# Attention values computed in pairs of column blocks, with some of their products in the seven-product form, and a new order of the stages around them

## The chip, the cores and the metric

The kernel runs on one core of a Trainium2 chip. The metric is the device time of one execution in microseconds (us). Three runs of the kernel before gave 2039.58, 2039.71 and 2039.95 us; the median, 2039.71 us, is the time to which the changed kernel is compared.

## The reference, cut to what matters

One layer of a hybrid block on x of 256 rows by 4096 columns, all in float32:

```
xn   = rms_norm(x)
proj = xn @ w_in                 # 4096 -> 14336: q, k, v, z_a, a_c, g_c, z_c, 2048 columns each
y_a  = attention(q, k, v)        # 16 heads of 128; here every query row sees the earlier chunks; a bias from rel_table
y_a  = rms_norm(y_a) * silu(z_a)
u    = a_c * sigmoid(g_c)
u    = depthwise_conv(u, 31 taps) # along the rows, channel by channel
y_c  = silu(layer_norm(u)) @ w_pw
y_c  = rms_norm(y_c) * silu(z_c)
h    = x + [y_a, y_c] @ w_out
h    = h + sigmoid(rms_norm(h) @ w_ple_gate + b) * (p @ w_ple)
out  = rms_norm(h)
```

## The kernel before, in words

**Products.** Every large product has 256 output rows (two halves of 128, called h), blocks of 512 output columns, and a depth of 4096 in 32 blocks of 128. To keep float32 accuracy each operand is split in a high part and a low part, and each product is made of three matmuls: high by high, low by high, high by low. The left operand (`xT`, transposed and split once) stays in memory; each weight block comes by DMA into a tile `wt` and is split there (`parts_of`, lines 199 to 209): ScalarE casts the high part (`wh`, line 204) and VectorE subtracts it from the weight to get the low part (`wl`, line 205).

There are two routines. `product` (line 224) makes one block of 512 columns: 32 depth blocks, two halves, three matmuls, so 192 matmuls (line 218). `mixed_product` (line 327) makes two column blocks at once and takes the depth in 16 pairs of blocks; an `order` says in which sequence and which pairs are "seven" pairs, marked with a star. A plain pair takes 24 matmuls, from two split weight tiles of 128x1024. A seven pair is a step of a Strassen-like scheme: seven products of 128-blocks in place of eight, 21 matmuls. It needs sums of weight blocks, `ua` and `ub` (VectorE, lines 426, 427, 430, 431), which are split as well (`uh`, `ul`, again lines 204 and 205), and combinations of left blocks that were made earlier. Four helper banks (P1, P5, P6, P7, shown as `acc_P`) are added up by VectorE after the last seven pair (`helper_sums`, lines 467 to 471). `scaled_pair` (line 478) wraps `mixed_product`: it takes two tiles `z` from `sum_tiles` (line 473, tag "stage"), puts the helpers' sums in, scales them, and at the end adds the four accumulators with four VectorE instructions (line 492).

**Stages.** The first third of the kernel makes, from `w_in`, for c and g from 0 to 3:

- `glu_conv(c)` (line 689): a `scaled_pair` for a_c and g_c, a sigmoid and a product, transposes, and 124 convolution taps of VectorE (`conv_tap`, lines 671 to 680), which are not issued but put into a list `later`;
- `heads(g)` (line 883): a DMA of the bias of four heads and a memset on GpSimd, a `scaled_pair` for queries and keys, `to_heads` (line 826: transposes into `qT` and `kT`, tag "hd"), one `product` for the values (line 903, two ScalarE copies at line 904), and `attention` (line 844), head after head, which writes into a new tile `y_a` (tag "act");
- `layer_norm_swish` (line 726), whose 71 steps (four idle ones among them at three places) also go into `later`.

The order is glu_conv(0), glu_conv(1), heads(0), glu_conv(2), heads(1), glu_conv(3), heads(2), layer_norm_swish, heads(3). Of glu_conv(3) six pairs are seven pairs (`early_six`, line 321), of the other pairs from glu_conv(1) on four (`early`, line 320). Then `w_pw` follows (line 956, order "1 3 4 5 0* 6 2* 7" for its first two column blocks); its operand `uS` is made by the last 16 steps of the layer norm.

**What sets the order.** Each product calls `fill(n)` after each pair (line 419 or 457; `product` at line 235, two for each two depth blocks), which takes n steps off `later`. `early_fills` (line 323) gives these numbers pair by pair; they add up to 64. The place at which a step is taken off gives its place in the program. A scheduler orders each engine's queue at compile time: it takes the ready instruction that stands first in the program, so later taps come forward where an engine would be idle. On the chip each queue runs in that fixed order. Tiles come from pools with tags: a tag has a fixed number of buffers (weight parts `wh` and `wl` 3 each, `uh` and `ul` 2 each, "hd" 5, the small PSUM tiles 4). The scratch pool `upool` is closed in heads(3) behind the keys, and a pool `more`, for `uS`, takes its place (lines 898 to 900). The pool `spool` is closed before `w_pw`, and `lpool` takes its place (line 937): from it come `ua` and `ub` of `w_pw` and its row of b_pw.

Of the kernel before, what the change touches and what calls it, by code (L numbers as in the profile page):

```python
# [25 lines left out]
def hybrid_block(  # L26
# [137 lines left out]
    def transposed(src, blocks, then=lambda ins: None):  # L164

        pt = tmp_psum()
        for i, b in enumerate(blocks):
            for h in range(NH):
                last_transpose[:] = [
                    nc.tensor.transpose(  # L170
                        pt[:, i * T + h * P : i * T + (h + 1) * P],
                        src[:, h, b * P : (b + 1) * P],
                        ident,
                    )
                ]
                then(*last_transpose)
        return [pt[:, i * T : (i + 1) * T] for i in range(len(blocks))]
# [143 lines left out]
    early_six = units("1 3 5 7 0* 9 2* 11 4* 13 6* 15 8* 10* 12 14")  # L321

# [175 lines left out]
    def square_sum(dst, src, scale=1.0):  # L498
        junk = spool.tile([P, NB], mybir.dt.bfloat16, tag="junk", name="junk", bufs=1)
        return nc.scalar.activation(junk[:, : src.shape[1]], src, AF.Square, scale=scale, accum_out=dst)  # L500
# [225 lines left out]
    def layer_norm_swish():  # L726
# [4 lines left out]
        def hd_tile(name):  # L731
            return spool.tile([P, 4, T], F32, tag="hd", name=name, bufs=5)

# [92 lines left out]
    def to_heads(st, name):  # L826

        t = spool.tile([P, GH, T], F32, tag="hd", name=name, bufs=5)
# [15 lines left out]
    def attention(g, qT, kT, v, bias):  # L844
        y = act.tile([P, NH, NB], F32, tag="act", name="y_a")
        for hd in range(GH):
# [28 lines left out]
            for h in range(NH):  # L875
                nc.scalar.activation(
                    y[:, h, vc], o[:, h * HD : (h + 1) * HD], AF.Identity, scale=den[:, h : h + 1]
                )
        for h in range(NH):
            square_sum(ssq_a[:, h, g : g + 1], y[:, h, :])  # L880
        y_a.append(y)

    def heads(g):
        nonlocal more
        bias = spool.tile([P, GH, T], F32, tag="hd", name="bias", bufs=5)
# [10 lines left out]
        q, k = scaled_pair(w_in0, o_q + g * NB, o_k - o_q, early, r_x, (4,) if g == n_g - 1 else early_fills)  # L896
        qT, kT = to_heads(q, "qT"), to_heads(k, "kT")
        if g == n_g - 1:
            first_sums.close()
            more = pool("more", 4)  # L900
        accv = product(w_in0, o_v + g * NB, xT, KD)
        v = spool.tile([P, NH, NB], F32, tag="hd", name="v", bufs=5)
        for h in range(NH):
            nc.scalar.activation(v[:, h, :], accv[h], AF.Identity, scale=r_x[:, h : h + 1])
        attention(g, qT, kT, v, bias)

    n_g = H // GH
    assert n_g == CW // NB
# [68 lines left out]
    def gated(ys, c0, col, r_y, order, ahead):  # L977
# [8 lines left out]
        for h, j in QUARTERS:  # L986
            zz, y = z[h][j], ys[c0 + j][:, h, :]
            tt(zz, acc[h][j], zz, ALU.subtract if j else ALU.add)
            nc.scalar.activation(zz, zz, AF.Silu, scale=r_x[:, h : h + 1])
            later.append(partial(stt, y, y, r_y[:, h : h + 1], zz, ALU.mult, ALU.mult))  # L990
# [280 lines left out]
```

## Time and profile before

| what | value |
|---|---|
| runs, median | 2039.71 us |
| the profiled execution, first to last instruction | 2038.9 us |
| TensorE (PE): busy, matmuls | 2021.0 us, 9106 |
| VectorE (DVE): busy | 1905.7 us |
| ScalarE (ACT): busy | 1184.3 us |
| GpSimd (POOL): busy | 8.1 us |
| read from device memory | 406.39 MB |

The profile has no total of its own for the profiled execution beyond its span; the median of the runs is 0.8 us above that span. PE stands for matmuls and PEld for the loads of their stationary operand. A matmul's duration in the profile has a modelled end; matmuls overlap, so the rate at which they follow each other is read from the chain, as its time divided by its count. VectorE's instructions overlap a little too, so a step's cost there is the distance between two starts.

### The profile page before, as it was taken

The numbers are of one execution on the slowest core, as the hardware profiler recorded it, in microseconds if no ns is written. First come the engines' busy times: TensorE is split into PE (matmuls) and PEld (weight loads), VectorE is DVE, ScalarE is ACT, GpSimd is POOL, SyncE is SP. The second block draws the span as 40 slices with busy tenths as digits, with TensorE's granted clock in tenths as the row PEclk, the third lists the DMA queues.
The fourth block names the chain that finished last, engine by engine and source line by source line (L and its number), as shares of the span: only waits on it lengthen the run. The fifth ranks groups of instructions, "written<-read, shape, count | busy, mean of one in ns | idle before, by whom it ended". The sixth has DMA issues, their size and how long they took to land.

```text
span 2038.9 us, 26038 instructions
## 1 busy us (share of the span) xinstructions
PE 2021.0 (99%) x9106; PEld 1661.3 (81%) x9106; DVE 1905.7 (93%) x2720; ACT 1184.3 (58%) x1527; POOL 8.1 (0%) x19
## 2 busy tenths in 40 slices
PE   9999999999999999999999999999999999999997
PEld 7888888887888888888888888888888888888876
DVE  7999999899989998878899999999999999999998
ACT  7655535554555545576555656676565666655555
POOL 0000000000000000000000000000000000000000
PEclk9999999999999999999999999999999999999999
DMA  8566665666656665556666666676666656666765
GB/s 294 188 198 204 200 191 167 203 191 186 184 178 211 202 184 186 178 192 197 187 216 206 197 214 201 215 243 204 211 205 205 206 190 208 198 222 205 234 206 180
DMA packets 161853, 412.29 MB, mean 202 GB/s; under 512 B 12974, under 2 KB 16190, under 8 KB 161722
## 3 DMA queue, kind: packets, MB, share of 16 engines
q1 hardware_dynamic: 161072, 409.80, 62.9%
q8 instruction: 71, 1.16, 0.2%
q10 hardware_dynamic: 650, 0.84, 0.1%
q14 instruction: 60, 0.49, 0.1%
HBM read 406.39 MB, written 4.19 MB: 201 GB/s over the span
## 4 chain that ended last, share of the span: by engine, by line
PE 86%; DVE 10%; issue 2%; ACT 1%; DMA 0%; POOLq 0%; POOL 0%; ACTq 0%; DVEq 0%
PE acc L370 60%; PE acc_P L370 15%; PE acc L218 8%; DVE wl L205 4%; DVE cv L677 3%; PE tmp_ps L170 1%; DVE ul L205 1%; ACT wh L204 0%; PE tmp_ps L834 0%; PE tmp_ps L849 0%; DVE ub L431 0%; PE tmp_ps L867 0%; DVE ub L430 0%; DVE ua L426 0%; DVE ua L427 0%
## 5 line engine op out<-in xcount | busy, mean ns | idle before, releaser
L370 PE MATMUL acc<-wh,big_t 128*128 128x512 f32 x3788 | 1173.6, 391 | 0.9 <-DVE y_c L964 0.7
L204 ACT CAST wh<-wt 128x1024 fp32r<-128x1024 f32 (+1 forms) x737 | 714.7, 980 | 558.4 <-PE acc L370 335.4
L205 DVE TENSOR_TENSOR wl<-wt,wh 128x1024 fp32r<-128x1024 f32 (+1 forms) x737 | 823.7, 1130 | 48.2 <-ACT wh L204 43.0
L370 PEld LDWEIGHTS acc<-wh,big_t 128*128 128x128 f32 x3788 | 708.2, 188 | 147.9 <-DVE y_c L964 1.1
L370 PE MATMUL acc<-wl,big_t 128*128 128x512 f32 x1894 | 730.7, 391 | 0.2 <-DVE wl L205 0.2
L370 PEld LDWEIGHTS acc<-wl,big_t 128*128 128x128 f32 x1894 | 355.2, 188 | 75.7 <-DVE wl L205 2.0
L677 DVE SCALAR_TENSOR_TENSOR cv<-uT,dw,cv 128x255 f32<-128x255 f32 (+20 forms) x480 | 205.1, 463 | 1.3
L204 ACT CAST uh<-ub 128x1024 fp32r<-128x1024 f32 x122 | 128.3, 1052 | 123.9 <-DVE ub L431 99.9
L218 PE MATMUL acc<-wh,big_t 128*128 128x512 f32 x560 | 173.9, 392 | 0.0
L204 ACT CAST uh<-ua 128x1024 fp32r<-128x1024 f32 x122 | 128.6, 1054 | 72.5 <-DVE ua L427 65.3
L205 DVE TENSOR_TENSOR ul<-ub,uh 128x1024 fp32r<-128x1024 f32 x122 | 148.8, 1219 | 7.7 <-ACT uh L204 6.9
L370 PE MATMUL acc_P<-uh,big_t 128*128 128x512 f32 x504 | 154.4, 392 | 0.1
L205 DVE TENSOR_TENSOR ul<-ua,uh 128x1024 fp32r<-128x1024 f32 x122 | 148.6, 1218 | 0.6 <-ACT uh L204 0.4
L218 PEld LDWEIGHTS acc<-wh,big_t 128*128 128x128 f32 x560 | 105.5, 189 | 21.6
L370 PEld LDWEIGHTS acc_P<-uh,big_t 128*128 128x128 f32 x504 | 93.5, 188 | 22.3 <-ACT uh L204 3.6
L218 PE MATMUL acc<-wl,big_t 128*128 128x512 f32 x280 | 109.6, 392 | 0.0
L426 DVE TENSOR_TENSOR ua<-wt 128x512 f32<-128x512 f32 x122 | 83.7, 686 | 26.3 <-DMA wt<-in_w_in_dram 21.4
L370 PE MATMUL acc_P<-ul,big_t 128*128 128x512 f32 x252 | 96.5, 391 | 0.0
L427 DVE TENSOR_TENSOR ua<-wt 128x512 f32<-128x512 f32 x122 | 83.4, 684 | 4.6 <-DMA wt<-in_w_in_dram 3.5
L431 DVE TENSOR_TENSOR ub<-ub,wt 128x512 f32<-128x512 f32 x122 | 83.6, 685 | 1.0
L430 DVE TENSOR_TENSOR ub<-ua,wt 128x512 f32<-128x512 f32 x122 | 83.4, 683 | 0.3
L370 PE MATMUL acc<-uh,big_t 128*128 128x512 f32 x244 | 75.4, 390 | 0.0
(241 smaller groups left out, 1526.4 us busy)
## 6 DMA issues: line engine op xcount, KB each, us to landing
wt<-in_w_in_dram SPq DMA_DIRECT2D x447, 512.0 KB, 4.1
wt<-in_w_out_dram SPq DMA_DIRECT2D x128, 512.0 KB, 4.1
wt<-in_w_ple_gate_dram SPq DMA_DIRECT2D x128, 512.0 KB, 4.2
wt<-in_w_pw_dram SPq DMA_DIRECT2D x32, 512.0 KB, 4.6
hc<-in_x_dram SPq DMA_DIRECT2D x8, 512.0 KB, 5.6
wt<-in_w_ple_dram SPq DMA_DIRECT2D x8, 512.0 KB, 4.4
xin<-in_x_dram SPq DMA_DIRECT2D x7, 512.0 KB, 8.3
out_dram<-hc SPq DMA_DIRECT2D x12, 256.0 KB, 2.5
```

Source lines behind the costliest of these rows:

```text
L170: nc.tensor.transpose(pt[:, i * T + h * P : i * T + (h + 1) * P], src[:, h, b * P : (b + 1) * P], ident,)
L204: nc.scalar.copy(wh[:, :kc, :], wt[:, :kc, :]),
L205: nc.vector.tensor_tensor(wl[:, :kc, :], wt[:, :kc, :], wh[:, :kc, :].bitcast(F32), ALU.subtract),
L218: nc.tensor.matmul(acc, a, b[:, k, :], start=kb == 0 and kind == 0, stop=kb == kblocks - 1 and kind == 2,)
L370: nc.tensor.matmul(banks[name], a, b, start=name not in begun, stop=final and ends[name] == n and kind == 2 and not (left and name in "P2 ...
L426: plus(ua[:, 0], w0[:, 0], w0[:, 1])
L427: plus(ua[:, 1], w0[:, 1], w1[:, 1])
L430: plus(ub[:, 0], ua[:, 0], w1[:, 1])
L431: plus(ub[:, 1], ub[:, 0], w1[:, 0])
L677: nc.vector.scalar_tensor_tensor(cv[:, i, PAD - k :], uT[:, i, : T + k - PAD], dw[:, b, k : k + 1], cv[:, i, PAD - k :], ALU.mult, ALU.add,)
```

## The change

It does these things:

- `values(g, ...)` makes the values of two column blocks (8 heads) with one `scaled_pair`: 16 pairs, 4 of them seven pairs. values(0) has `early` and `early_fills`, values(2) a new order `valued` and fills of its own (their sum is 58). The values then lie in the tiles `z`, for values(0) with the tag "hd", for values(2) "stage".
- `qT` is taken from the pool "act", and attention writes its result over it, head by head; the squares and the later readers take it as a tile of four dimensions.
- The order is glu_conv(0), glu_conv(1), bias 0, keys(0), values(0), attention(0), glu_conv(2), glu_conv(3), bias 1, keys(1), attention(1), keys(2), layer_norm_swish, keys(3), values(2), attention(2), attention(3).
- Biases 2 and 3 are loaded, `upool` closed and `more` opened behind the last seven pair of values(2) (`late_pool`).

```
+    valued = units("1 3 5 7 8 0* 9 2* 10 4* 11 6* 12 13 14 15")
...
-    def sum_tiles():
+    def sum_tiles(**kw):
+        kw = kw or dict(tag="stage")
-        t = [spool.tile([P, NH, NB], F32, tag="stage", name="z") for _ in range(2)]
+        t = [spool.tile([P, NH, NB], F32, name="z", **kw) for _ in range(2)]
...
-    def scaled_pair(w, col, apart, order, r, fills, **kw):
+    def scaled_pair(w, col, apart, order, r, fills, home={}, then=lambda: None, **kw):
         def on_helpers(helper):
-            for dst, src in zip((t, z), sum_tiles()):
+            for dst, src in zip((t, z), sum_tiles(**home)):
                 dst.extend(src)
+            then()
...
-    def attention(g, qT, kT, v, bias):
-        y = act.tile([P, NH, NB], F32, tag="act", name="y_a")
+    def attention(g):
+        qT, kT, v, bias = qs[g], ks.pop(g), vs.pop(g), biases.pop(g)
+        y = qT.rearrange("q g (h d) -> q h g d", h=NH)
...
+    def keys(g, fills):
+        q, k = scaled_pair(w_in0, o_q + g * NB, o_k - o_q, early, r_x, fills)
+        qs[g] = act.tile([P, GH, T], F32, tag="act", name="qT")
+        to_heads(q, qs[g])
+        ks[g] = hd_tile("kT")
+        to_heads(k, ks[g])
+
+    def values(g, order, fills, **kw):
+        vs[g], vs[g + 1] = scaled_pair(w_in0, o_v + g * NB, NB, order, r_x, fills, **kw)
+
+    def late_pool():
+        nonlocal more
+        first_sums.close()
+        more = pool("more", 4)
+        for g in (2, 3):
+            load_bias(g)
...
     glu_conv(0)
-    for g in range(n_g):
-        if g + 1 < n_g:
-            glu_conv(g + 1)
-        else:
-            layer_norm_swish()
-        heads(g)
+    glu_conv(1)
+    load_bias(0)
+    keys(0, early_fills)
+    values(0, early, early_fills, home=dict(tag="hd", bufs=5))
+    attention(0)
+    glu_conv(2)
+    glu_conv(3)
+    load_bias(1)
+    keys(1, early_fills)
+    attention(1)
+    keys(2, early_fills)
+    layer_norm_swish()
+    keys(3, (4,))
+    values(2, valued, (5, 5, 4, 5, 4, 2, 3, 2, 3, 2, 3, 4, 4, 4, 4, 4), then=late_pool)
+    attention(2)
+    attention(3)
```

More of the change, by code (lines that the diff above doesn't have):

```diff
@@ L171, in transposed @@
                         pt[:, i * T + h * P : i * T + (h + 1) * P],
-                        src[:, h, b * P : (b + 1) * P],
+                        src[:, h, b] if len(src.shape) == 4 else src[:, h, b * P : (b + 1) * P],
                         ident,
@@ L876, in attention, with hd_tile, load_bias @@
                 nc.scalar.activation(
-                    y[:, h, vc], o[:, h * HD : (h + 1) * HD], AF.Identity, scale=den[:, h : h + 1]
+                    y[:, h, hd], o[:, h * HD : (h + 1) * HD], AF.Identity, scale=den[:, h : h + 1]
                 )
         for h in range(NH):
-            square_sum(ssq_a[:, h, g : g + 1], y[:, h, :])
+            square_sum(ssq_a[:, h, g : g + 1], y[:, h])
         y_a.append(y)
-    def heads(g):
-        nonlocal more
-        bias = spool.tile([P, GH, T], F32, tag="hd", name="bias", bufs=5)
+    qs, ks, vs, biases = {}, {}, {}, {}
+    def hd_tile(name):
+        return spool.tile([P, GH, T], F32, tag="hd", name=name, bufs=5)
+    def load_bias(g):
+        bias = biases[g] = hd_tile("bias")
         span = 2 * MAXR + 1
@@ L895, in heads @@
         nc.gpsimd.memset(bias[: P // 2, :, : P // 2], NEG)
[L896 to L905, printed above, removed]
+    def keys(g, fills):
[12 more added lines that the diff above has]
+            load_bias(g)
     n_g = H // GH
-    assert n_g == CW // NB
+    assert n_g == CW // NB == 4
     glu_conv(0)
-    for g in range(n_g):
-        if g + 1 < n_g:
-            glu_conv(g + 1)
-        else:
-            layer_norm_swish()
-        heads(g)
+    glu_conv(1)
[14 more added lines that the diff above has]
+    attention(3)
     r_a = rstd_of(ssq_a, AW, "r_a")
```

12 lines of the change are left out of this document (6 added, 6 removed).

## The prediction

> **What bounds the kernel now.** I read the page first: busy times, chain, groups.
>
> ```profile
> PE 2021.0 (99%) x9106; PEld 1661.3 (81%) x9106; DVE 1905.7 (93%) x2720; ACT 1184.3 (58%) x1527; POOL 8.1 (0%) x19
> ...
> PE 86%; DVE 10%; issue 2%; ACT 1%; DMA 0%; POOLq 0%; POOL 0%; ACTq 0%; DVEq 0%
> ...
> L204 ACT CAST uh<-ub 128x1024 fp32r<-128x1024 f32 x122 | 128.3, 1052 | 123.9 <-DVE ub L431 99.9
> L218 PE MATMUL acc<-wh,big_t 128*128 128x512 f32 x560 | 173.9, 392 | 0.0
> ```
>
> TensorE sets the end, and VectorE has little to spare. ScalarE (58%) has much. Busy PE is modelled, so I take the rate from the chain in order of time, once in a values product (L218) and once in a mixed one (L370):
>
> ```profile
> 273.61 43.12 PE acc L218 x190
> ...
> 380.70 31.96 PE acc L370 x141
> ```
>
> 43.12/190 = 31.96/141 = 0.2267 us a matmul, in both forms. A plain pair is then 24 x 0.2267 = 5.44 us of PE, a seven pair 4.76.
>
> The windows by stage show where VectorE has room (columns: length, busy and instructions of PE, PEld, DVE, ACT, POOL, then clock, DMA share and GB/s). They are glu_conv(1), keys(0), values(0) and glu_conv(3), then the four heads of attention(3):
>
> ```profile
> 103.10:190.80 87.70, 87.57 (x390) 71.09 (x387) 87.18 (x139) 44.71 (x50) 0.00 (x0) 1.00 0.62 193
> 190.80:273.40 82.60, 82.27 (x373) 68.05 (x371) 82.16 (x132) 42.20 (x46) 0.31 (x1) 1.00 0.67 208
> 273.40:316.50 43.10, 43.10 (x192) 35.68 (x191) 43.06 (x79) 16.24 (x16) 0.00 (x0) 1.00 0.63 191
> 567.00:639.00 72.00, 72.00 (x321) 59.55 (x320) 60.00 (x69) 43.77 (x52) 0.00 (x0) 1.00 0.62 195
> 904.20:926.00 21.80, 21.80 (x119) 17.68 (x117) 15.05 (x32) 14.73 (x33) 0.00 (x0) 1.00 0.44 150
> ```
>
> To see: from 103 to 316 both engines are full. glu_conv(3) leaves VectorE 12 us free; the same window for line 677 alone says why: no tap is left there.
>
> ```profile
> 567.00:639.00 72.00, 0.00 (x0) 1.00 0.62 195
> ```
>  Over the whole region:
>
> ```profile
> 103.00:930.00 827.00, 824.06 (x3744) 677.68 (x3743) 767.07 (x1234) 440.89 (x571) 2.69 (x6) 1.00 0.61 190
> ```
>
> VectorE is idle for 60 of 827 us. That is the room from which the change has to live. The price of its steps is the distance between starts, from the timeline of keys(0):
>
> ```profile
> 234.37 0.69 DVE L426 TENSOR_TENSOR ua<-wt 128x512 f32<-128x512 f32 x1
> 234.97 0.69 DVE L427 TENSOR_TENSOR ua<-wt 128x512 f32<-128x512 f32 x1
> ...
> 239.43 1.22 DVE L205 TENSOR_TENSOR ul<-ub,uh 128x1024 fp32r<-128x1024 f32 x1
> 240.57 0.47 DVE L677 SCALAR_TENSOR_TENSOR cv<-uT,dw,cv 128x248 f32<-128x248 f32 x1
> ```
>
> 0.60 us for 512 columns and 1.14 for 1024; a tap takes 0.38 (four in 1.51 us, in the timeline quoted below).
>
> **The change, part by part.**
>
> *Fewer matmuls.* L218 counts 560 with `wh`, which are two of each three, so 840: 4 x 192 = 768 for values and 72 for the embedding. Two column blocks cost 384 now; with four seven pairs 12 x 24 + 4 x 21 = 372. Twice 12 matmuls go: 24 x 0.2267 = **-5.4 us**. Nothing else on PE changes in number.
>
> *More work for VectorE.* A plain pair costs it 2 x 1.14 = 2.28 us, as in the values of before. A seven pair costs three of 1024 and five of 512, 3.4 + 3.0 = 6.4. Eight seven pairs add 8 x 4.1 = 33 us. Helper sums (4 x 0.60) and accumulators (4 x 0.66, from 2.73 for four in a row below), which ScalarE copied before, add 2 x 5.0. Together +43 us. With PE's 5.4 us less, 60 - 43 - 5 = 12 us of room stay in the region, so the place counts. Balances by stage:
>
> - A `scaled_pair` with four seven pairs holds VectorE 12 x 2.28 + 4 x 6.4 + 5.0 = 58 us, and 64 taps add 24.4: 82.4 against 372 x 0.2267 = 84.3 of PE. So values(0) runs as keys(0) does, where both were full and PE lost almost nothing. Cost 0; if it loses, 1 us (82.60 above holds 371 matmul loads, 84.1 us at the rate; the borders blur it by that).
> - values(2) has the layer norm for a fill, of which a keys stage with layer norm in it shows the load:
>
> ```profile
> 783.00:860.00 77.00, 77.00 (x350) 63.80 (x349) 67.13 (x88) 45.44 (x54) 0.70 (x1) 1.00 0.61 192
> ```
>
>   10 us of 77 are free there; cost 0, and 2 us if its steps wait on each other.
> - glu_conv(3) is the weak place. Before, its own taps and those of glu_conv(2) lay apart by keys, values and attention. Now it follows glu_conv(2) directly, so 60 taps of glu_conv(2) stand in it (64 fills less 4 of combinations), and nothing could be done ahead.
>
> The last six pairs of `early_six` are three seven and three plain: PE 3 x 4.76 + 3 x 5.44 = 30.6 us. VectorE 3 x 6.4 + 3 x 2.28 = 26.0, with 28 taps (2+4+6+6+6+4) 10.7 and helper sums 2.4: 39.1. That is 8.5 us too much; the two combinations in place of four taps add 2.5 further ahead (each two steps of 512 and four of 128, which I estimate at half a tap: 2.0), so 11. How much of it PE feels depends on the lead and on whether taps give way. The lead, at the last seven pair of glu_conv(1), on DVE and on PE:
>
> ```profile
> 149.22 0.68 DVE L205 TENSOR_TENSOR wl<-wt,wh 128x512 fp32r<-128x512 f32 x1
> ```
> ```profile
> 153.82 0.61 PE L370 MATMUL acc_P<-uh,big_t 128*128 128x512 f32 x2
> ...
> 157.17 0.62 PE L370 MATMUL acc<-uh,big_t 128*128 128x512 f32 x2
> 157.63 0.41 PE L370 MATMUL acc_P<-ul,big_t 128*128 128x512 f32 x1
> ```
>
> P1's three matmuls stand ahead of the first of these, so the pair begins at 153.1: a lead of 4 us, just enough, as P6's `ul` comes when it is needed. And taps give way only one for one, as at the start of glu_conv(1), where 18 are due before the first seven pair:
>
> ```profile
> 109.02 0.69 DVE L426 TENSOR_TENSOR ua<-wt 128x512 f32<-128x512 f32 x1
> 109.63 0.47 DVE L677 SCALAR_TENSOR_TENSOR cv<-uT,dw,cv 128x251 f32<-128x251 f32 x1
> 110.02 1.22 DVE L205 TENSOR_TENSOR wl<-wt,wh 128x1024 fp32r<-128x1024 f32 x1
> ```
>
> So the stall lies between 0 (all gives way) and 11 us (nothing does). The nearest row is this yielding by halves; I take the middle, **+5.5 us**.
>
> *Ends of stages.* Before, one end cost something: after keys(1), transposes waited for VectorE, which did four taps ahead of the accumulators (timeline), and the granted clock fell (window).
>
> ```profile
> 493.50 1.60 DVE L677 SCALAR_TENSOR_TENSOR cv<-uT,dw,cv 128x228 f32<-128x228 f32 x4
> 495.01 2.73 DVE L492 SCALAR_TENSOR_TENSOR z<-acc,r_x,z 128x512 f32<-128x512 f32 x4
> ```
> ```profile
> 494.00:502.00 8.00, 6.30 (x28) 4.84 (x27) 8.00 (x13) 1.04 (x1) 0.00 (x0) 0.79 0.24 70
> ```
> ```profile
> PE tmp_ps L834 <- DVE z L492: 1.9, 3, 1.3
> ```
>
> A wait of 1.3 us, and 8 x 0.21 = 1.7 us by the clock: 3.0. Four such ends remain, in another rhythm. None again is -3.0, a second one +3.0. I take half of it gone, **-1.5 us**. The row shows a lower clock after a short wait. The Trainium skill ("TensorE: Matmul & The Clock Gate", section "HAM oscillation — how this bites in real kernels") gives gaps of over some 3.4 us as the limit; by it, stalls of 1 to 3 us in glu_conv(3) cost only themselves, by the row each may cost 1.7 us more. The measurement stands against the page here, and neither is in the sum.
>
> *Attention(2) and (3) in a row.* On PE a head needs others' matmuls between its steps. How many went there, windows of line 370 alone show, for the four heads of attention(3) and for the last three of attention(2), where VectorE had little else:
>
> ```profile
> 904.20:925.90 21.70, 17.91 (x65) 11.76 (x65) 1.00 0.44 150
> 768.80:782.60 13.80, 11.22 (x39) 7.03 (x39) 1.00 0.53 176
> ```
> ```profile
> 928.31 0.80 SPq L923 DMA_DIRECT2D row<-in_b_pw_dram  x2
> 928.39 0.69 DVE L426 TENSOR_TENSOR ua<-wt 128x512 f32<-128x512 f32 x1
> ```
>
> So 65 for four heads and 13 for each of the next four, 117. The four plain pairs of `w_pw` give 96. Its first seven pair can't begin before `lpool` is free: `ua` starts at 928.4, 2.4 us behind the last head, with which the window above ends, and until its parts are ready another 3 us, 24 matmuls, are wanted. 141 less 96 is 45 matmuls, 10.2 us, at worst. But P2 and P3 of that pair (6) and the plain pair behind it (24) need only weight parts; the swap at 157.17, where a later matmul goes ahead of `ul`, shows that the order does such things. 15 would be lacking, 3.4 us, though a head speeds up where PE is free. Between 0 and 10.2 I take **+0.5**, near the row of attention(2), which ran its heads with 13.
>
> *Nothing for the rest.* ScalarE gets at most 8 x 2 casts of 1.05 us more, hidden at 58% busy; uncovered 17 us. Writing over `qT` waits only for matmuls long done. Biases 2 and 3 go out in the middle of values(2): behind them in SyncE's queue stand the weights of its last four pairs, 21.8 us of PE, and GpSimd's memset, behind which nothing stands. Up to two weight tiles are already there. Should a bias wait for a buffer, PE runs dry after one pair; I cost it 0, at worst one landing time, 6.7 us:
>
> ```profile
> bias<-in_rel_table_dram SPq DMA_DIRECT2D x4, 512.0 KB, 6.7
> ```
>
> `more` opens later, but 16 splits of `uS` have four pairs and two attentions left.
>
> Sum: 2038.9 - 5.4 + 5.5 - 1.5 + 0.5 = 2038.0 for the span, and the runs' median lies 0.8 above it: **2038.8 us**, no change within 0.2% (4.1 us, about what a measurement of this kernel can tell).
>
> **Rivals.**
>
> *The overload is not felt* (faster). glu_conv(3) hands its taps on, since VectorE had 12 us free there and later stages 1 to 2 us each. For it: the one-for-one yielding. Against: no such slack is left behind it before values(2). -5.4 - 1.5 + 0.5: 2033.3; with no stage end stalling 2031.8. Chance 0.31.
>
> *VectorE becomes the bound in glu_conv(3)* (slower). One mechanism: parts of 8* and 10* come late by the whole overload, and the clock falls once. -5.4 + 11 + 1.7 + 0.5 - 1.5 = +6.3: 2046.0. It decides for slower from a stall of 10.5 us on (5.4 + 1.5 - 0.5 + 4.1). For it: taps stand first in program order. Chance 0.14.
>
> *Two attentions run out of matmuls* (slower). 10.2 us in place of 0.5: 2048.5; slower from 5.5 us on, that is when under 21 matmuls are brought forward. Chance 0.11.
>
> *The order doesn't hold*: the layer norm isn't done behind values(2), and `w_pw` waits. What it would wait for are at most the 16 last subtractions:
>
> ```profile
> L803 DVE TENSOR_TENSOR big_t<-cv,big_t 128x256 fp32r<-128x256 f32 x16 | 5.7, 416 | 0.0
> ```
>
> +5.7, 2044.5. Chance 0.02.
>
> **How the numbers follow.** Forecast 0.42, its own range 2035.6 to 2042.9. Faster 0.32 (first rival and an edge of the forecast), within 0.2% 0.42, slower 0.26. The range for 8 in 10 runs from 2031.8 to 2046.5: all of the first rival, the forecast, and the middle of the slower ones.
>
> **What would show it.** 9082 matmuls. In glu_conv(3), waits of acc and acc_P for DVE `ul` and `wl`, and a window in which VectorE is full while PE counts fewer than 4.4 matmuls a us; without them the first rival is right. Behind values(2), eight heads in about 40 us with PE unbroken, and `ua` of `w_pw` 2.4 us behind the last head. A fall of the clock at an end of keys. I am wrong if values(0) itself loses time, or if a DMA ends a wait in values(2).

## The result, and the profile after

The changed kernel takes 2051.41 us (median of 5 runs, 2049.85 to 2053.13) against 2039.58 us of the kernel before: 1.0057 times, 95% interval 1.0046 to 1.0068. A second measurement of it (e5 below) gave 1.0044, 1.0032 to 1.0057. It is slower by 8 to 12 us where about 1 us less was forecast, and the first median lies 5 us above the range. As the same kernel gave 1.0057 and 1.0044, a difference of 0.001 between two kernels that were not measured together says little.

The page of the profile after, with the lines that answer to those of before: engines, chain, one group.

```profile
PE 2021.3 (99%) x9082; PEld 1652.6 (81%) x9082; DVE 1944.7 (95%) x2784; ACT 1196.2 (58%) x1543; POOL 8.1 (0%) x19
...
PE 87%; DVE 8%; issue 2%; DMA 1%; ACT 1%; SPq 0%; POOL 0%; POOLq 0%; ACTq 0%; DVEq 0%
...
L204 ACT CAST uh<-ub 128x1024 fp32r<-128x1024 f32 x130 | 136.9, 1053 | 125.5 <-DVE ub L433 105.1
```

The 24 matmuls are gone (9106 to 9082), the eight more seven pairs are there (`ub` 122 to 130), VectorE has 39 us more. From line 322 on its lines are numbered 1 to 25 higher (L370 is L372 now, L677 is L682). Shares this flat don't tell where 10 us went. The stages do. First the large stretch: GpSimd's small instructions on `r_x` (in glu_conv(0)) and `r_c` (behind `w_pw`) are marks that both kernels have. Before:

```profile
60.94 1.01 POOL L139 TENSOR_TENSOR r_x<-r_x,mhalf 128x2 f32<-128x2 f32 x1 [59.49 <-DVE r_x L138]
...
1002.32 0.69 POOL L139 TENSOR_TENSOR r_c<-r_c,mhalf 128x2 f32<-128x2 f32 x1 [72.02 <-DVE r_c L138]
```

After:

```profile
62.30 1.01 POOL L139 TENSOR_TENSOR r_x<-r_x,mhalf 128x2 f32<-128x2 f32 x1 [60.85 <-DVE r_x L138]
...
1010.76 0.69 POOL L139 TENSOR_TENSOR r_c<-r_c,mhalf 128x2 f32<-128x2 f32 x1 [65.35 <-DVE r_c L138]
```

From `r_x` to `r_c` it was 941.4 us and is 948.5: +7.1, although 5.4 us of matmuls went. So some 12.5 us are lost inside. (Another 1.4 us at the start and 2.5 behind `r_c` were not seen in e5: there the marks of the same kernel stand at 60.90 and 1008.35, a stretch of 947.5, in a span of 2045.3. Their cause is open.) All experiments below are compared by this stretch too; it is that of one profiled execution each.

Windows of after: values(0), glu_conv(2), and 48 us of glu_conv(3).

```profile
273.40:357.30 83.90, 83.90 (x377) 69.53 (x376) 83.80 (x133) 41.65 (x44) 0.00 (x0) 1.00 0.63 195
...
382.00:454.00 72.00, 72.00 (x322) 59.73 (x321) 63.65 (x90) 39.92 (x49) 0.00 (x0) 1.00 0.62 190
...
500.00:548.00 48.00, 42.69 (x183) 32.64 (x181) 47.83 (x76) 25.56 (x29) 0.31 (x1) 1.00 0.59 181
```

values(0) runs with both engines full, as forecast. In glu_conv(2) VectorE is idle for 8 us. In glu_conv(3) it is full, and PE gets through 183 matmuls in 48 us, where 48 / 0.2267 = 212 would fit. The waits of PE in that place (total, times, longest):

```profile
PE acc_P L372 <- ACT uh L204: 4.3, 3, 2.4
PE acc L372 <- DVE wl L205: 1.1, 2, 0.6
```

ScalarE's `uh` is named, but it only casts what VectorE's sums `ua` and `ub` give it. VectorE's timeline there shows why they come late: a tap stands before each of them.

```profile
513.88 0.68 DVE L428 TENSOR_TENSOR ua<-wt 128x512 f32<-128x512 f32 x1
514.49 0.47 DVE L682 SCALAR_TENSOR_TENSOR cv<-uT,dw,cv 128x251 f32<-128x251 f32 x1
514.88 0.68 DVE L429 TENSOR_TENSOR ua<-wt 128x512 f32<-128x512 f32 x1
515.48 0.47 DVE L682 SCALAR_TENSOR_TENSOR cv<-uT,dw,cv 128x250 f32<-128x250 f32 x1
```

The second place is the end of the stretch, the eight heads and `w_pw`. Windows of line 372 alone: two heads in a row, then the 30 us behind the last head; and in before the same 30 us (line 370).

```profile
904.60:909.60 5.00, 2.02 (x6) 1.05 (x6) 1.00 0.07 16
909.60:914.90 5.30, 4.38 (x16) 2.86 (x16) 1.00 0.82 270
...
939.80:969.80 30.00, 28.45 (x121) 22.07 (x122) 1.00 0.62 216
```
```profile
926.00:956.00 30.00, 29.84 (x129) 24.06 (x130) 1.00 0.65 211
```

The second of the eight heads has 6 matmuls of others beside it, the third 16, in nearly the same time: a head does not get shorter where PE is free. Behind the last head PE does 8 fewer than before. What ScalarE did ahead of the second head (L804 is a split of the layer norm's result):

```profile
898.82 2.85 ACT L804 CAST big_t<-cv 128x256 fp32r<-128x256 f32 x9
901.58 2.94 ACT L204 CAST wh<-wt 128x1024 fp32r<-128x1024 f32 x3
```

The layer norm's last steps, which before lay in values(3), now lie among the first heads. VectorE makes the last of their subtractions at 906.53 and only then, at 906.86, the next `wl` of `w_pw`: that is in the second head. (The first head begins at 887.05, beside the last 60 matmuls of values(2), which end at 902.) The waits of PE that the profile names from 880 to 975 us come to 3.2 us, the longest 1.1 us (for `y_c`): no single wait makes this loss.

### The profile page after: what moved, and what is told of

The parts are those of the page before. It is cut to its first block, busy times and chain, and to the rows that moved or that the text cites. A ratio compares the mean times of both kernels' runs of the same rounds, so it can differ in the third digit from the quotient of the medians.

```text
span 2049.8 us, 26039 instructions
## 1 busy us (share of the span) xinstructions
PE 2021.3 (99%) x9082; PEld 1652.6 (81%) x9082; DVE 1944.7 (95%) x2784; ACT 1196.2 (58%) x1543; POOL 8.1 (0%) x19
## 4 chain that ended last, share of the span: by engine, by line
PE 87%; DVE 8%; issue 2%; DMA 1%; ACT 1%; SPq 0%; POOL 0%; POOLq 0%; ACTq 0%; DVEq 0%
PE acc L372 68%; PE acc_P L372 15%; DVE wl L205 3%; DVE cv L682 1%; DVE ul L205 1%; PE tmp_ps L170 1%; DMA wt<-in_w_in_dram 1%; PE acc L218 1%; DVE ub L433 0%; DVE ub L432 0%; PE tmp_ps L835 0%; PE tmp_ps L851 0%; DVE ua L428 0%; PE tmp_ps L869 0%; DVE ua L429 0%
## 5 line engine op out<-in xcount | busy, mean ns | idle before, releaser
L372 PE MATMUL acc<-wh,big_t 128*128 128x512 f32 x4196 | 1296.4, 392 | 4.0 <-DVE wh L563 1.6
L372 PEld LDWEIGHTS acc<-wh,big_t 128*128 128x128 f32 x4196 | 784.2, 188 | 168.5 <-ACT big_t L156 2.4
L372 PE MATMUL acc<-wl,big_t 128*128 128x512 f32 x2098 | 804.0, 391 | 2.0 <-DVE wl L205 1.8
L372 PEld LDWEIGHTS acc<-wl,big_t 128*128 128x128 f32 x2098 | 393.0, 188 | 87.1 <-DVE wl L205 5.7
L682 DVE SCALAR_TENSOR_TENSOR cv<-uT,dw,cv 128x255 f32<-128x255 f32 (+22 forms) x480 | 213.1, 463 | 1.0
L372 PE MATMUL acc_P<-uh,big_t 128*128 128x512 f32 x528 | 161.7, 393 | 0.0
L205 DVE TENSOR_TENSOR ul<-ua,uh 128x1024 fp32r<-128x1024 f32 x130 | 158.6, 1220 | 0.9 <-ACT uh L204 0.2
L372 PEld LDWEIGHTS acc_P<-uh,big_t 128*128 128x128 f32 x528 | 97.4, 188 | 24.3 <-ACT uh L204 5.0
L428 DVE TENSOR_TENSOR ua<-wt 128x512 f32<-128x512 f32 x130 | 89.3, 687 | 21.8 <-DMA wt<-in_w_in_dram 15.0
L372 PE MATMUL acc_P<-ul,big_t 128*128 128x512 f32 x264 | 101.1, 394 | 1.0 <-DVE ul L205 1.0
L429 DVE TENSOR_TENSOR ua<-wt 128x512 f32<-128x512 f32 x130 | 89.1, 685 | 2.3 <-DMA wt<-in_w_in_dram 1.3
L372 PE MATMUL acc<-uh,big_t 128*128 128x512 f32 x260 | 80.6, 390 | 0.0
L372 PE MATMUL acc_P<-wh,big_t 128*128 128x512 f32 x260 | 80.6, 389 | 0.0
L372 PE MATMUL acc_P<-uh,comb_t 128*128 128x512 f32 x228 | 70.1, 392 | 0.2
L372 PEld LDWEIGHTS acc_P<-ul,big_t 128*128 128x128 f32 x264 | 49.2, 188 | 15.2 <-DVE ul L205 4.9
```

The lines of the kernel that those rows point to most:

```text
L205: nc.vector.tensor_tensor(wl[:, :kc, :], wt[:, :kc, :], wh[:, :kc, :].bitcast(F32), ALU.subtract),
L372: nc.tensor.matmul(banks[name], a, b, start=name not in begun, stop=final and ends[name] == n and kind == 2 and not (left and name in "P2 ...
L428: plus(ua[:, 0], w0[:, 0], w0[:, 1])
L429: plus(ua[:, 1], w0[:, 1], w1[:, 1])
L682: nc.vector.scalar_tensor_tensor(cv[:, i, PAD - k :], uT[:, i, : T + k - PAD], dw[:, b, k : k + 1], cv[:, i, PAD - k :], ALU.mult, ALU.add,)
```

## The experiments

Two theories. **Two places**: the new order itself makes both losses; in glu_conv(3) the taps of glu_conv(2) can't be done ahead, and behind values(2) eight heads want more matmuls of others than there are. **VectorE short**: the seven pairs of the values take VectorE's room, and the loss shows wherever its lead runs out. "Stretch" is `r_x` to `r_c` of the profiled execution (941.4 before).

| run | matmuls | times before [95%] | stretch, us |
|---|---|---|---|
| e5 changed kernel again | 9082 | 1.0044 [1.0032, 1.0057] | 947.5 |
| e1 four | 9088 | 1.0030 [1.0018, 1.0041] | 942.7 |
| e2 ahead | 9082 | 1.0046 [1.0033, 1.0060] | 946.8 |
| e3 no variance | 9074 | 1.0064 [1.0052, 1.0077] | 951.3 |
| e4 plain first | 9082 | 1.0064 [1.0052, 1.0077] | 950.9 |
| e6 spread | 9082 | 1.0048 [1.0036, 1.0061] | 948.2 |
| e7 spread, four | 9088 | 1.0022 [1.0012, 1.0032] | 944.3 |
| e8 spread, ahead, four | 9088 | 1.0037 [1.0024, 1.0049] | 943.8 |
| e9 values(0) alone | 9094 | 1.0015 [1.0006, 1.0024] | 941.3 |
| e10 values(2) alone | 9094 | 1.0018 [1.0009, 1.0027] | 941.8 |
| e11 apart | 9082 | 1.0052 [1.0039, 1.0065] | 950.5 |
| e12 spread, four, gentle | 9088 | 1.0034 [1.0021, 1.0047] | 946.2 |
| e13 after, fewer taps | 9082 | 1.0013 [1.0004, 1.0022] | 943.1 |
| e14 before, fewer taps | 9106 | 0.9995 [0.9986, 1.0004] | 941.1 |
| e15 values(0), four | 9100 | 0.9981 [0.9972, 0.9990] | 935.7 |
| e16 order only | 9106 | 1.0078 [1.0065, 1.0090] | 954.9 |
| e17 order, plain w_pw | 9112 | 1.0045 [1.0032, 1.0057] | 946.8 |
| e18 values(0), five | 9097 | 0.9987 [0.9978, 0.9996] | 935.1 |

**One place at a time.** e1 takes glu_conv(3)'s two additional seven pairs away:

```
-                w_in0, o_a + c * NB, o_g - o_a, early_six if last else early, r_x, early_fills,
-                ahead=more_combinations if last else None,
+                w_in0, o_a + c * NB, o_g - o_a, early, r_x, early_fills,
```

> The changed kernel, but glu_conv(3) has four seven pairs in place of six and so no combinations; 6 more matmuls, 1.4 us. Overload theory (VectorE is given 60 taps in glu_conv(3) beside six seven pairs, so TensorE waits for uh and ul of 8* and 10*, 7.8 us): the waits go, and the time falls by 5 to 7 us, to 2044 to 2046 us. Rival, that glu_conv(3) only shows where VectorE's sum over the whole region is too large: the stall turns up again in keys(1) to keys(3), and the time falls by 2 us at most.

Measured: 2043.92 us. The same window, 48 us of glu_conv(3) in e1:

```profile
500.00:548.00 48.00, 48.00 (x216) 39.31 (x215) 47.48 (x79) 25.67 (x29) 0.30 (x1) 1.00 0.64 206
```

PE is whole, 216 matmuls in place of 183: 33 x 0.2267 = 7.5 us were lost there (a little less, as the count holds some short transposes), and VectorE is still nearly full. The overload is shown, and it lies in this stage. By its times, 1.0030 against 1.0044 and 1.0057, e1 gains only 3 to 5.5 us: it makes 1.4 us more of matmuls, and from 880 to 975 us PE waits 3.0 us for `wh`, where the changed kernel waits 0.4.

e2 puts glu_conv(2) ahead of values(0), so that glu_conv(3) no longer follows it:

```
     keys(0, early_fills)
+    glu_conv(2)
     values(0, early, early_fills, home=dict(tag="hd", bufs=5))
     attention(0)
-    glu_conv(2)
     glu_conv(3)
```

> The changed kernel, but with glu_conv(2) ahead of values(0) and attention(0); no instruction more or less. VectorE had 8 us without work in glu_conv(2), since all taps were done; now the taps of glu_conv(2) are there in time for values(0), and some 20 are done ahead of glu_conv(3). Overload theory: glu_conv(3) stalls 0 to 2 us in place of 7.8, the time falls by 5 to 8 us, to 2043 to 2046 us. Rival (the place of the stages is not the cause): within 1 us of 2051.

Measured: 2046.94 us, 1.0046 times before: next to e5 no gain. PE's waits for `uh` in glu_conv(3) fell from 4.3 to 1.0 us, as taps of glu_conv(2) could now be done ahead. But the 89 us from 886 on, the changed kernel and then e2, hold 12 matmuls fewer in e2:

```profile
886.00:975.00 89.00, 85.84 (x410) 67.73 (x409) 77.40 (x145) 61.95 (x127) 1.06 (x1) 1.00 0.50 169
```
```profile
886.00:975.00 89.00, 84.56 (x398) 66.69 (x397) 73.20 (x134) 52.03 (x102) 1.06 (x1) 0.98 0.47 161
```

In e2 the first two heads run with 20 and 16 matmuls beside them, and the last one with 7. What was won in one place was lost in the other.

e3 leaves out the small matmuls of the layer norm's variance and its spread, which need a small PSUM bank, and e4 puts the two seven pairs of `w_pw` last:

```
-            m = tmp_psum()
-            for h in range(NH):
-                nc.tensor.matmul(
...
-            rsqrt(st["r"], m[:, :NH], 1)
+            rsqrt(st["r"], s[:, :NH], 1)
```

> The changed kernel without the matmuls of the layer norm's variance and its spreading (two small matmuls each, in PSUM); the scale comes straight from memory, so the layer norm's result is another. Bank theory: the variance waits for a small PSUM bank until the four helpers of values(2) are read (it runs at 874 us, its sums were ready at 850), and swish and splits pile up on ScalarE and VectorE where attention(2) begins; without it they run 20 us earlier, and the time falls by 3 to 5 us. Rival, that attention(2) and (3) lack matmuls between their steps: within 1 us of 2051.

```
-    point = units("1 3 4 5 0* 6 2* 7"), units("0 1 2 3 4 5 6 7")
+    point = units("1 3 4 5 6 7 0* 2*"), units("0 1 2 3 4 5 6 7")
```

> The changed kernel, but the first two column blocks of w_pw take their six plain pairs first and the two seven pairs last: 144 matmuls in place of 96 are free of the pool that waits for attention(3). Theory of the missing matmuls: the waits in and behind attention(3) go, the time falls by 2 to 5 us. Bank theory (the loss is where attention(2) begins, not where attention(3) ends): it falls by 1 us or not at all.

Measured: 2050.65 and 2050.15 us, no gain by either. In e3 the layer norm is done earlier and the first two of the eight heads run clean; then these waits stand at the end (PE, 880 to 975 us):

```profile
PE acc L372 <- DVE y_c L977: 1.4, 1, 1.4
PE acc_P L372 <- ACT wh L204: 1.1, 1, 1.1
PE tmp_ps L866 <- DVE pT L863: 0.7, 1, 0.7
PE acc L372 <- ACT wh L204: 0.6, 1, 0.6
```

In e4 one wait of 3.1 us for the eviction `y_c` takes the place of what the longer supply brought. So the loss at the end is not one wait that can be taken out; it moves.

**The two attentions apart.** e5 is the changed kernel itself.

> The changed kernel once more, beside the three that follow, so that they can be compared with it on the same chip. 1.0057 times the kernel before, within its interval of 1.0046 to 1.0068. Region from r_x to r_c again 948 to 951 us (941.4 before).

e6 makes values(2) and attention(2) right behind keys(2), and the layer norm in keys(3) (cut; the loads of the biases move too):

```
     keys(2, early_fills)
-    layer_norm_swish()
-    keys(3, (4,))
-    values(2, valued, (5, 5, 4, 5, 4, 2, 3, 2, 3, 2, 3, 4, 4, 4, 4, 4), then=late_pool)
+    values(2, early, early_fills, home=dict(tag="hd", bufs=5))
     attention(2)
+    layer_norm_swish()
+    keys(3, (5, 5, 5, 5, 4, 5, 4, 5, 4, 5, 4, 4, 4, 4, 4, 4), then=late_pool)
     attention(3)
```

> values(2) and attention(2) stand right behind keys(2), then layer norm, keys(3) and attention(3): the two attentions are no longer in a row, and heads 8 to 11 get the plain pairs of keys(3) beside them. 9082 matmuls as in the changed kernel; glu_conv(3) is as in it. Theory 'two attentions in a row': the 6 to 7 us lost between values(2) and w_pw go, 5 to 7 us less than the changed kernel, about 1.0028 times before (2043 where before is 2037.6); the losses in glu_conv(3), 9 us, stay. Rival 'VectorE has too much to do in the whole region, and the loss only moves': within 2 us of the changed kernel, with the loss in another stage.

e7 is e6 with the edit of e1, e8 is e7 with that of e2:

> e6 with e1 (four seven pairs in glu_conv(3), in the plain order, and no combinations ahead of them): 9088 matmuls, 1.4 us more of TensorE. Theory 'two separate causes': both gains, 12 to 14 us less than the changed kernel, 0.9980 to 1.0000 times before (2034 to 2038 where before is 2037.6); region 934 to 938. Rival 'VectorE has too much to do in the whole region': at best one of the two gains, 2041 to 2044.

> e7 with glu_conv(2) ahead of values(0), so that values(0), its attention and two stages of four seven pairs share the taps of glu_conv(2) and (3) otherwise. Theory 'two separate causes', in which glu_conv(3) has nothing left to lose by e1: within 2 us of e7. Rival 'it is the place of the taps': another 3 to 4 us less than e7, about 0.9975 times before.

Measured: e5 2047.85, e6 2048.67, e7 2044.03, e8 2046.75 us. e6 misses its gain altogether, and e7 is little more than e1's gain. e8 lies above e7, which neither theory expected. Behind the last head nothing is lost any more in e6, but keys(3) pays; in e7 PE waits there 4.2 us for one cast of weights, on ScalarE:

```profile
878.43 4.02 ACT L793 ACTIVATE cv<-cv,prm 128x256 f32<-128x256 f32 x8
882.36 1.03 ACT L204 CAST wh<-wt 128x1024 fp32r<-128x1024 f32 x1
```

Eight swish instructions of the layer norm (L793) stand ahead of the cast in ScalarE's queue. This spoke for the rival, so one pair of values at a time comes next.

**One pair of values at a time.** e9 has values(0) as a pair in the order of before, values(2) and (3) by `product`; e10 the reverse, with the changed kernel's end. The edit of e9, cut:

```
     attention(0)
     glu_conv(2)
-    glu_conv(3)
     load_bias(1)
     keys(1, early_fills)
     attention(1)
+    glu_conv(3)
...
+    values_of(2)
     attention(2)
...
+    values_of(3)
     attention(3)
```

> Only values(0) made as a pair; values(2) and values(3) by product, and the order of the kernel before otherwise (glu_conv(2), keys(1), attention(1), glu_conv(3), keys(2), values 2, attention(2), layer norm, keys(3), values 3, attention(3)). 9094 matmuls. Theory 'two places': both losses of the changed kernel (glu_conv(3) directly behind glu_conv(2), and the end behind values(2)) are avoided, and the 12 matmuls saved are felt: 2.7 us less than before, less 1 for the rest, 0.9987 to 0.9997 times before; region from r_x to r_c 938.7 to 940 (941.4 before). Rival 'VectorE is short in the whole region': its 21 us of added work are felt somewhere, 1.000 to 1.002 times before.

> Only values(2) made as a pair with the changed kernel's end (keys(2), layer norm, keys(3), values(2), attention(2), attention(3)); values(0) and values(1) by product, in the order of before. 9094 matmuls. Theory 'two places': glu_conv(3) loses nothing, the end loses 6 to 7 us and gains 2.7: 1.0015 to 1.0025 times before, region 944.5 to 946. Rival 'VectorE is short in the whole region': as e9, 1.000 to 1.002, with the loss spread over stages.

e11 is e6 with glu_conv(3) behind attention(1) and the layer norm otherwise spread in keys(3); e12 is e7 with that spread:

```
-    keys(3, (5, 5, 5, 5, 4, 5, 4, 5, 4, 5, 4, 4, 4, 4, 4, 4), then=late_pool)
+    keys(3, (7, 7, 7, 7, 6, 2, 2, 2, 2, 3, 3, 4, 4, 5, 5, 5), valued, then=late_pool)
```

> Both pairs of values by seven products as in the changed kernel (9082 matmuls), but apart: glu_conv(3) behind keys(1) and attention(1), as before; values(2) and attention(2) right behind keys(2); the layer norm in keys(3), with an order and fills that bring its first 34 steps ahead of the first seven pair. Theory 'two places': the 24 matmuls saved are felt, 5.4 us less than before but for 1 to 3 of stage ends: 0.9975 to 0.999 times before. Rival 'VectorE is short in the whole region': 1.001 to 1.004 times before, and the losses stand again at other places.

> e7 with the layer norm spread otherwise in keys(3): the order of pairs and the fills of e11. In e7 one wait of 4.4 us stood in keys(3) at 878.8, where ScalarE had eight swish instructions ahead of the cast of the next weights. If that is the cause, it goes and e12 is 3 to 4 us below e7, 1.000 to 1.001 times before. If the layer norm costs that much wherever it stands, the wait comes back at another place and e12 is within 1.5 us of e7.

Measured: e9 2041.51, e10 2042.25, e11 2049.18, e12 2044.90 us. e10's time came as the theory of two places said: with 12 matmuls (2.7 us) fewer it is 3.7 us slower, so 6.4 us are lost, and its waits from 850 us on are those of the changed kernel. (Its stretch, from an execution 1.7 us under the median, is 941.8 where 944.5 to 946 was expected.) e9 and e11 did not, and e11 is slower than either theory said: glu_conv(3) loses again although keys(1) and attention(1) stand between it and glu_conv(2). 48 us of it in e9, and e9's waits from 570 to 700 us:

```profile
600.00:648.00 48.00, 45.29 (x192) 35.32 (x191) 48.00 (x75) 26.34 (x31) 0.31 (x1) 0.96 0.62 194
```
```profile
PE acc_P L372 <- ACT uh L204: 3.2, 3, 2.3
```

So the direct neighbourhood of glu_conv(2) is not what matters. Nor did the gentle spread help: in e12 waits of 3.1 us for `wh` and 2.7 for `wl` stand in place of e7's one of 4.2. That is the rival's picture, a loss that comes back elsewhere.

**Work and order apart.** e13 and e14 leave 112 of the 496 taps out of the changed kernel and of the kernel before:

```
-                later.append(partial(conv_tap, cv, uT, i, 4 * c + i, k))
+                left_out = k != PAD and k % 4 == 2
+                later.append((lambda: None) if left_out else partial(conv_tap, cv, uT, i, 4 * c + i, k))
```

> The changed kernel with 7 of the 30 later taps of each channel block left out (112 of 496; the steps stay in the list as empty ones, so all places in the program stay): about 43 us of VectorE's work less, which is what the change adds to it. The convolution is incomplete. Theory 'VectorE is short in the whole stretch': the losses in glu_conv(3) and at the end both go, 14 to 17 us less than the changed kernel, and 4 to 5.4 us less than e14. Theory 'two places' with causes of their own: glu_conv(3) is relieved (9 us less), but the end behind values(2), where no tap stands any more, keeps its 6 to 7 us: 1 to 3 us above e14.

> The kernel before with the same 112 taps left out, as the mark for e13. Both theories: 0 to 4 us less than before, as only the wait at the end of keys(1) (3 us) can go: 0.998 to 1.000.

e15 is e9 with the edit of e1:

> e9 (only values(0) as a pair, the order of before) with four seven pairs in glu_conv(3) in place of six: 9100 matmuls. In e9 glu_conv(3) lost some 7 us although keys(1) and attention(1) stood ahead of it. Theory 'VectorE is short in the whole stretch': that loss goes for 1.4 us more of TensorE, 4 to 6 us less than e9, 0.998 to 1.000 times before. Rival: the loss moves into keys(2) and attention(2): within 2 us of e9.

e16 keeps the changed order and takes the seven pairs of the values out of it (cut):

```
-        vs[g], vs[g + 1] = scaled_pair(w_in0, o_v + g * NB, NB, order, r_x, fills, **kw)
+        acc = mixed_product(w_in0, o_v + g * NB, xT, xS, plain, None, ahead=make, fills=fills, apart=NB)
+        for h, j in QUARTERS:
+            nc.scalar.activation(z[1][h][j], acc[h][j], AF.Identity, scale=r_x[:, h : h + 1])
```

> The changed kernel with all 16 pairs of values(0) and values(2) plain: the order, the places of the loads and of the pool are those of the change, the matmuls (9106) and VectorE's work those of before (ScalarE scales the accumulators, as it did before). Theory 'VectorE is short in the whole stretch': within 2 us of before, 0.999 to 1.001. Theory 'two places' (glu_conv(2) and (3) in a row, two attentions in a row): 6 to 10 us above before, 1.003 to 1.005.

Measured: e13 2040.86, e14 2037.77, e15 2034.56, e16 2053.74 us. **e16 decides.** With VectorE's work as before (2720 instructions in both) the order alone costs 0.78%, more than the whole change; the seven pairs then give back 0.21 to 0.34%, 4 to 7 us, about the forecast 5.4. e13 agrees: with VectorE as busy as in before (1905.9 us against 1905.7), the changed kernel is still 3.1 us above e14, and 5.4 + 3.1 = 8.5 us are still lost. The waits for `uh` in glu_conv(3) fell there from 4.3 to 0.8 us; those from 850 us on stayed. (e15 came as "VectorE short" said, but by taking the overload out of one stage.) "VectorE short" falls as the cause of the total. Only how the order acts in glu_conv(3) was wrong in the theory of two places. e16's windows show it, glu_conv(2) and glu_conv(3), then the taps alone (line 683 here) in glu_conv(2):

```profile
382.00:454.00 72.00, 72.00 (x319) 59.60 (x319) 50.92 (x55) 39.27 (x47) 0.00 (x0) 1.00 0.61 190
500.00:548.00 48.00, 42.97 (x183) 33.00 (x182) 47.81 (x76) 25.08 (x28) 0.09 (x1) 1.00 0.60 185
```
```profile
382.00:454.00 72.00, 0.00 (x0) 1.00 0.61 190
```

In glu_conv(2) VectorE is idle for 21 us of 72 without one tap: those of glu_conv(0) and (1) are all done, and those of glu_conv(2) exist only at its end. Then glu_conv(3) loses exactly what it loses in the changed kernel, 183 matmuls in 48 us. It is the **supply of taps**, not VectorE's total work: room that lies ahead of the taps is worth nothing. e2, which makes these taps earlier, bears it out, with the waits for `uh` at 1.0 us. In before the products values(0) and values(1) lay between the glu stages, and VectorE did taps ahead of their turn in their room: 58 in values(0) alone (line 677, window of before), where the fills asked for 32.

```profile
273.40:316.50 43.10, 22.97 (x58) 1.00 0.63 191
```

e9 took the product values(1) out from between glu_conv(2) and (3), and so 40 taps were left for the window of glu_conv(3) that in before held none (line 682):

```profile
567.00:639.00 72.00, 18.17 (x40) 0.98 0.57 177
```

At the end of e16, behind the last head (its last two matmuls, then `w_pw`):

```profile
946.33 0.39 PE L877 MATMUL tmp_ps<-z,pT 128*128 128x128 f32 x2
946.48 0.71 PE L373 MATMUL acc_P<-wh,big_t 128*128 128x512 f32 x2
947.02 0.40 PE L373 MATMUL acc_P<-wl,big_t 128*128 128x512 f32 x1
948.55 0.74 PE L373 MATMUL acc_P<-wh,big_t 128*128 128x512 f32 x2 [1.13 <-ACT wh L204]
```

The first seven pair (`acc_P`) begins right behind the last head. Nothing of it was drawn forward, and the last head had 7 matmuls beside it, the seven pair's first among them (window 941.90 to 946.50, line 373):

```profile
941.90:946.50 4.60, 1.76 (x7) 1.18 (x7) 1.00 0.24 89
```

The waits from 880 to 975 us are those of e3, one by one: 1.4 for `y_c`, 1.1 and 0.6 for `wh`, 0.7 for `pT`. e2 has the same four. In these three kernels the first head begins only behind values(2), so that all eight live on matmuls of `w_pw`. They have 120 of them, the 96 and the 24 of the plain pair behind the seven pair, and end in the same way, with none left.

**More matmuls, and five pairs.** e17 is e16 with more of them:

```
-    point = units("1 3 4 5 0* 6 2* 7"), units("0 1 2 3 4 5 6 7")
+    point = units("1 3 4 5 6 7 0 2"), units("0 1 2 3 4 5 6 7")
```

> e16 with the first two column blocks of w_pw all plain (order 1 3 4 5 6 7 0 2): 9112 matmuls, 1.4 us more of TensorE, but twice as many matmuls that the eight heads may draw on, and no helper banks or sums wanted behind the last head. Theory 'eight heads run out of matmuls' (in e16 the heads 9 to 14 had 13 to 18 matmuls beside them, the last one 6, and behind it 6.9 us were lost, before 1.0): head 15 gets 13 or more and the loss behind it falls by 4 to 6 us: 2 to 5 us less than e16. Rival, an end that pays elsewhere (a late eviction of y_c, the heads themselves): within 1.5 us of e16 or above it.

e18 is e15 with a fifth seven pair in glu_conv(3) (the edit as it stands against the changed kernel, cut):

```
-    early_six = units("1 3 5 7 0* 9 2* 11 4* 13 6* 15 8* 10* 12 14")
+    early_six = units("1 3 5 7 0* 9 2* 11 4* 13 6* 15 8* 10 12 14")
-        if pair in (7, 9):
+        if pair == 7:
```

> e15 with five seven pairs in glu_conv(3) (8* kept, 10 plain, its combination left out): 9097 matmuls, 0.7 us less than e15. With six (e9) glu_conv(3) lost 7 us, with four nothing. If the overload grows with each pair from the start, half the loss comes back: 2 to 4 us above e15. If there is room for one more, 0 to 0.7 us below it, 0.9975 to 0.998 times before.

Measured: e17 2046.29, e18 2034.69 us. The 89 us from 886 on, e16 and then e17:

```profile
886.00:975.00 89.00, 84.30 (x398) 65.23 (x397) 67.97 (x125) 53.24 (x109) 1.06 (x1) 1.00 0.44 154
```
```profile
886.00:975.00 89.00, 89.00 (x433) 72.55 (x433) 62.03 (x119) 54.87 (x107) 0.72 (x1) 1.00 0.50 173
```

35 matmuls more in the same time, and from 880 to 975 us not one wait of PE. The stretch falls by 954.9 - 946.8 = 8.1 us (by the ratios 6.7), with 1.4 us more of matmuls: 9.5 us of e16's loss are gone. The last head of e17 takes no longer with 14 matmuls beside it than e16's with 7 (line 373):

```profile
940.10:944.90 4.80, 3.80 (x14) 2.44 (x14) 1.00 0.30 109
```

So the places were there for PE to fill. e17 also wants no sums of weights, no helper banks and less of VectorE at that place (62.03 us against 67.97); how much of the 9.5 us is the lack of matmuls alone was not separated. e4, which only moves the seven pairs behind the plain ones, gained nothing: its last two heads had 17 each, and 3.1 us went into the wait for `y_c`. The edit of e17 on the changed kernel was not tried.

e15 and e18 beat both kernels, the one before by 0.1 to 0.2%: one pair of values, the order of before, four or five seven pairs in glu_conv(3). The window that held 192 matmuls in e9 holds, in e15 and in e18:

```profile
600.00:648.00 48.00, 48.00 (x217) 39.77 (x217) 44.52 (x72) 23.77 (x26) 0.31 (x1) 1.00 0.65 203
```
```profile
600.00:648.00 48.00, 48.00 (x216) 39.21 (x215) 47.93 (x78) 26.13 (x30) 0.30 (x1) 1.00 0.66 214
```

With five VectorE is full (47.93 of 48.00) and PE loses nothing; with six it loses 25 matmuls, 5.7 us. In this order the overload begins at the sixth.

## Why the prediction was wrong, step by step

The stretch as the runs give it: 941.4 - 5.4 + 7.5 - 3.0 + 8.0 = 948.5, the last term by difference (7.0 by e5; e10, which has this end alone, lost 6.4 us by its time).

- **Fewer matmuls, -5.4**: right, and felt. 9082 counted; e16 against the changed kernel shows about that much.
- **values(0), 0**: right; PE 83.90 of 83.90 us in its window, clock 1.00. No DMA ends a wait of PE in values(2), and the biases cost nothing.
- **glu_conv(3), +5.5**: the mechanism right, the size low. 7.5 us of the 11 that "nothing gives way" would cost. Its bounds were worked out from the last six pairs; that the rest of the stage brings no relief was said rightly ("nothing could be done ahead"). Under 4.4 matmuls per us was the sign: 183 / 48 = 3.8. The longest waits were for `uh`, not for the `ul` and `wl` that the prediction named.
- **End of keys(1), -1.5**: both the wait of 1.3 us and the fall of the clock there are gone, so -3.0, the lower bound. No other end of keys took its place.
- **Attention(2) and (3) in a row, +0.5: this step failed.** 6 to 8 us were lost from values(2) on. The sum set the matmuls that are wanted (117 beside the heads, 24 behind the last) against those that there are (96, and 30 brought forward). It let 0.5 stand for the 3.4 us that still lacked, near a row of 13 a head and as "a head speeds up where PE is free". It does not: 4.8 us with 14 matmuls in e17, 4.6 with 7 in e16, 5.0 with 6 in the changed kernel. And 117 was too few: in e17, where none lack, it is 126, 13 to 19 a head. Nine more make 5.4 us of lack by the prediction's own count. What was to be brought forward came for the most part: in e16 the 24 of the plain pair beside the last heads, in the changed kernel P2, P3 and 18 of the plain pair behind the last head (940.53 to 946), while `ua` came 3.8 us behind that head (943.50) in place of 2.4.
- **The layer norm behind values(2), 0: wrong too.** The 16 splits of `uS`, which had "four pairs and two attentions left", stand among the first two heads, and so the second head got 6 matmuls. It is the largest single piece of the loss that the changed kernel's trace shows: 8 fewer than the heads behind it have, 1.8 us. The rest is spread over waits of 1.1 us and less; how the 6 to 8 us divide between late operands and lacking matmuls stays open. The sign "eight heads in about 40 us" did not show it, as they ended 38 us behind values(2), with the first half done by then; but PE was not unbroken.
- **The rivals.** "VectorE becomes the bound" was true, 7.5 of 11 us, and the clock did not fall in the changed kernel. "Two attentions run out of matmuls" had the size, some 8 of 10.2 us, and in e2, e3 and e16 the mechanism; in the changed kernel a part of it is "The order doesn't hold" (chance 0.02), the layer norm not done behind values(2). Each was priced with the other at its forecast value, so as if only one could happen. They lie in different stages, and they add: 2038.9 - 5.4 + 7.5 - 3.0 + 8.0 = 2046.0 for the span, 2046.8 with the 0.8 around it, just beyond the range. What is left up to the profiled 2049.8 are the 3.8 us outside the stretch, which e5 does not show.

## What to carry to other kernels

Work that fills gaps has a date from which it exists: check for each stage not only how much room an engine has but which fillers have been issued by then (in e16 21 us of VectorE lay idle one stage ahead of the overload). The same holds for the matmuls beside a serial chain: count what stands behind it up to the first instruction that can't be moved, and whether its operands are ready by then. Where two stages are put together, price the two losses as a sum, and test an order without the saving that it was made for: here the order cost 15 us and the saving paid 5 of them.

## What the runs showed of the hardware

The granted clock fell after some waits and not after longer ones. The stall of glu_conv(3) is nearly the same in e9 and in the changed kernel. e9, 4 us from its wait of 2.3 us on:

```profile
616.00:620.00 4.00, 3.45 (x11) 2.75 (x12) 4.00 (x7) 1.81 (x3) 0.00 (x0) 0.75 0.43 131
```

The changed kernel, over its two waits of 2.4 and 1.6 us:

```profile
523.00:527.00 4.00, 1.90 (x8) 1.60 (x9) 4.00 (x7) 2.10 (x2) 0.00 (x0) 1.00 0.42 124
527.00:531.00 4.00, 2.37 (x10) 1.62 (x10) 4.00 (x6) 1.05 (x1) 0.00 (x0) 1.00 0.32 74
```

18 matmuls in 8 us, half of the full rate, and the clock stays at 1.00; in before it fell to 0.79 around a wait of 1.3 us. e17 is the same program as e16 up to `w_pw`. Over this stall e16's clock stayed at 1.00 (from 527 to 531 us 11 matmuls), and e17's fell:

```profile
527.00:531.00 4.00, 3.96 (x11) 2.59 (x11) 4.00 (x7) 1.17 (x2) 0.00 (x0) 0.60 0.28 79
```

So the length of a wait does not settle it here. The Trainium skill ("TensorE: Matmul & The Clock Gate", section "Part 1: The HAM clock gate (the "warmup" mystery)") says that activity is watched in a window of about 3.4 us that runs freely and does not start anew with a kernel. That would fit e16 and e17, as one and the same stall can fall inside one window or across two; no run here shows the window itself. The rule of the Trainium skill ("TensorE: Matmul & The Clock Gate", section "HAM oscillation — how this bites in real kernels"), that there should be no gaps of over some 3.4 us, is not enough here: the clock fell after waits of 1.3 us in before and 2.3 us in e9.
